# A hybrid encoder block on one core: q and k rows interleaved, and the second MLP stage in a written order on the first stage's tiles

## The chip, the core and the metric

The kernel runs on one core of a Trainium2 chip. Five engines work side by side, each through its own instructions in order: PE (TensorE: matmul), DVE (VectorE), ACT (ScalarE), POOL (GpSimd) and SP (SyncE, which here only issues transfers). They wait for each other through semaphores. The metric is the device time in microseconds (us); lower is better.

## The reference, cut to what matters

One layer on x of 1024 tokens by 1024 features, all in float32:

```python
h = rmsnorm(x, norm_mix_w)
z, xbc, dt_raw, q, k, v = jnp.split(h @ w_in, offs, axis=-1)
y_ssm = ssd_mixer(z, xbc, dt_raw, ...)            # conv, two-way chunked scan, gate, norm
y_na = neighbourhood_attention(q, k, v, ...)      # 16 heads of 64, q and k normed per head
x = x + jnp.concatenate([y_ssm, y_na], -1) @ w_out
h = rmsnorm(x, norm_mlp_w)
return x + jnp.square(jax.nn.relu(h @ w_mlp_in)) @ w_mlp_out   # 1024 -> 4096 -> 1024
```

In the attention each token sees a window of 8 rows by 16 columns of the 16 x 64 grid, with a bias per head.

## The kernel before, in words

**Number format.** Every float32 operand of a matmul is split into a high part (`hi`, made by ACT at L369) and a low part (`lo`, made by DVE or POOL at L370 as the difference), and a product is three matmuls: hi·hi, hi·lo, lo·hi. The helper `split_to(hl, src, eng)` does one such split of a 128 x 1024 tile; `eng` says who makes the low part. Weights are split with POOL, activations with DVE.

**Stages in time.** 0 to about 200 us: the norm of x, projections of x, B, C, dt, convolution. Up to about 610 us: the pieces of z, q, k, v and the scan. About 610 to 890 us: attention, interleaved with the first three quarters of the output projection. About 890 to 975 us: its last quarter, the second norm and the first blocks of the MLP. About 975 to 1270 us: the first MLP matmul (stage 1). From then to the end: the second (stage 2).

**Attention.** It goes over 8 pairs of heads, p = 0 to 7, in two rounds of tiles (`q0`/`q1`, and so on). q, k and v were stored to DRAM by the projection stage (ACT's queue issues those stores) and `pair_loads` (L412 on) brings a pair back: q in 4 transfers of 256 KB, each to 64 partitions, one per half of the tile and of the parts (hi, lo); k in 2 transfers of 512 KB, each to 64 partitions (head j to partitions 64j to 64j+63); the low part of k, `kl`, in 2 of 256 KB to 64 partitions; v in one of 1 MB to 128 partitions. For a head the tile `q[:, j]` holds on its 128 partitions one block of 64 rows with the high part and one with the low part, and `k[:, j]` the same rows of k twice, so that one matmul (L1401) sums two of the three terms; a second one with `kl` (L1402), whose other half is zero (set by POOL at L442, in the first round), adds the third. Scores `psc` are shifted by a bias `mb` and their maxima taken (DVE, L1405), exponentiated (ACT, L1417), turned by PE (L1429), split (`pth`, ACT L1441; `ptl`, DVE L1439) and multiplied with v (L1369). The bias comes from DRAM (`braw`) and is added to a mask by POOL (L1336). The output weights `wraw` are loaded by SP (L500) and split by ACT (`wh`, L507) and POOL (`wl`, L510) for the projection matmuls `po` (L364 to L366).

**What sets the order up to 975 us.** A planner takes tasks with a cost for their engine, tiles, readers and due times and makes a list; `in_order()` fixes each engine's instructions in the order of that list. A load is one task on SP (`load_task`), so all loads, of whatever tile, have the line L397.

**The MLP.** Each stage is a blocked product of 2 x 2 blocks done with 7 products instead of 8 (`ORD = (1, 2, 6, 5, 7, 3, 4)`); sums and differences of blocks are made by DVE. Stage 1 has 8 blocks `fb` of 512 hidden features. A product is 24 matmuls. `Block.split(i)` makes the differences of the weights it needs and splits one tile; `Block.product(i)` issues the matmuls; `Block.sums(i)` takes the PSUM results (ACT copies, L1628, or DVE adds, L1633), applies relu and square (ACT, L1639) and, for products 3 and 4, makes the combinations that stage 2 wants (DVE, L1646 to L1654) and stores them to `act_dr`. Stage 2 has 4 parts of 7 products, 48 matmuls each: two tiles of weights and two of activations are needed for a product. Weights are loaded to `wraw` tiles and combined by DVE (L1915, L1916, L1918, L1920); activations are loaded (`ar`) and split (`ahl`, with DVE); the PSUM results are added to `acc`, which starts as the residual x2 (L1945). After stage 1 the pool `b0s` is closed, and stage 2 opens pools of its own. From 975 us on, a scheduler of the compiler's front end sets the order on each engine; nothing in the kernel's text fixes it.

Of the kernel before, what the change touches and what calls it, by code (L numbers as in the profile page):

```python
# [10 lines left out]
F32 = mybir.dt.float32  # L11
# [219 lines left out]
def hymba_block(  # L231
# [64 lines left out]
    q_dr = dr.tile([2, 2, 4, P, T], F32, name="q_dr")  # L296
# [113 lines left out]
    def pair_loads(plan, p, after=()):  # L410
# [4 lines left out]
        qp = {(j, a): part(q) for j in range(2) for a in range(2)}  # L415
        kp = [part(k) for _ in range(2)]
        for j in range(2):
            for a in range(2):
                load_task(
                plan,  # L420
                    256,
                    partial(lambda j, a: q.t[a * HD : (a + 1) * HD, j].bitcast(F32), j, a),
                    partial(lambda j, a: q_dr[p // 4, a ^ j, p % 4, j * HD : (j + 1) * HD], j, a),
                    reads=after, writes=[qp[j, a]],
                    name="q",
                    since=-10.0 if p == 1 else -1e3,
                )
            load_task(
                plan,
                512,  # L430
                partial(lambda j: k.t[j * HD : (j + 1) * HD].bitcast(F32), j),
                partial(lambda j: k_dr[p // 4, 0, p % 4].rearrange("(h d) t -> d h t", h=2), j),
                reads=after, writes=[kp[j]],
                name="k",
                **free,
            )
        if p < 2:
            kls[p] = Buf(f"kl{i}"), []
            for j in range(2):
                half_, whole = part(kls[p][0]), kls[p][0]  # L440
                kls[p][1].append(half_)
                task("POOL", 1.0, partial(lambda j, b: nc.gpsimd.memset(b.t[HD * (1 - j) : HD * (2 - j), j].bitcast(F32), 0.0), j, whole), writes=[half_], name="kl0", **free)  # L442
        kl, klp = kls[i]
        for j in range(2):
            hp = slice(HD * j, HD * j + HD)
            load_task(plan, 256, partial(lambda hp, j: kl.t[hp, j].bitcast(F32), hp, j), partial(lambda hp: k_dr[p // 4, 1, p % 4, hp], hp), reads=after, writes=[klp[j]], name="kl", **free)
# [11 lines left out]
    def handed_on(plan, loaded):  # L458

        Buf, part = plan.buf, plan.part  # L460
        q, k, kl, v = (plan.given(Buf(b.tag), b.t) for b in (loaded[0], loaded[2], loaded[4], loaded[6]))
        qp = {(j, a): part(q) for j in range(2) for a in range(2)}
        kls[0] = kl, [part(kl) for _ in range(2)]
        return q, qp, k, [part(k) for _ in range(2)], *kls[0], v
# [56 lines left out]
    with ExitStack() as ph:  # L521
# [375 lines left out]
        def piece(j, b):  # L897
# [28 lines left out]
            to, w = (q_dr, 80) if kind(j) == "q" else (k_dr, 81)  # L926
# [6 lines left out]
            def turn():  # L933
                for i in range(4):
# [10 lines left out]
                    to[g, :, :, :, s].rearrange("a p f t -> f (a p) t"),  # L945
# [242 lines left out]
        def in_order():  # L1188
# [4 lines left out]
            for ins in traced[start:]:  # L1193
                if ins.engine in behind:
# [49 lines left out]
    with ExitStack() as ph:  # L1244
# [107 lines left out]
        def attend(H, mb, loaded, yT, yparts, den, dens):  # L1352
# [39 lines left out]
            for b in range(NT):  # L1392
# [51 lines left out]
                task("PE", 2 * (n / 2400 + 0.014), scores, reads=[qp[hh, 0], qp[hh, 1], *kp, klp[hh]], writes=[pt], due=due(b), name="psc")  # L1444
# [101 lines left out]
    with ExitStack() as ph:  # L1546
# [283 lines left out]
        for fb in range(8):  # L1830
# [13 lines left out]
    b0s.close()  # L1844

    with ExitStack() as ph:
        phase["ps"] = ph.enter_context(
            tc.tile_pool(name="ps4", bufs=1, space=PSUM, reuse_waits="tile")
        )
        ra, wa_, rb, x0, wb_, a2, a1, arb = (  # L1850
            ph.enter_context(tc.tile_pool(name=n, bufs=1, side="right", reuse_waits="tile"))
            for n in ("ra", "wa", "rb", "x0", "wb", "a2", "a1", "arb")
        )
        x1, a3 = (
            ph.enter_context(tc.tile_pool(name=n, bufs=1, reuse_waits="tile")) for n in ("x1", "a3")
        )
        acc = [p.tile([P, NT // 2, D], F32, name="acc") for p in (x0, x1)]
        hls[:] = [wa_] * 2 + [wb_] * 2 + [wp] * 3
        raw_a = [arp] * 2 + [ra] * 4
        raw_b = [rb] * 6 + [wp] * 2  # L1860
        raw_x = [arp] * 2 + [arb] * 2
        ahl = [a1] * 2 + [a2] * 2 + [a3] * 2
        for n in ("hl", "raw", "rb", "ar", "ahl"):
            ring[n] = 0

        def raw_of(n):
            if n in ("11", "21"):
                return ring_tile("raw", raw_a, ("wraw",), (F32,))[0]
            return ring_tile("rb", raw_b, ("wraw",), (F32,))[0]

        def a_load(fb, i, u):
            ar = ring_tile("ar", raw_x, ("ar",), (F32,))[0]
            nc.sync.dma_start(
                ar.rearrange("p (a t) -> p a t", a=2), act_dr[fb][i - 1, :, 2 * u : 2 * u + 2, :]
            )
            return ar

        def a_split(ar):
            pool = ahl[ring["ahl"] % 6]
            ring["ahl"] += 1  # L1880
            t = pool.tile([P, 2, 1024], F32R, tag="ahl", name="ahl", bufs=2)
            split_to((t[:, 0], t[:, 1]), ar, nc.vector)
            return t[:, 0], t[:, 1]

        for fb in range(4):
            bq = [{}, {}]
            for n in ("11", "21", "12", "22"):
                for q in bq:
                    q[n] = raw_of(n)
            first = {}  # L1890
            with ExitStack() as order:
                if fb == 1:
                    order.enter_context(tc.issue_after(begun.ins))
                for n in ("11", "21", "12", "22"):
                    for u in range(2):
                        r0 = (2 * fb + u) * 512 + (int(n[0]) - 1) * 256
                        d0 = (int(n[1]) - 1) * 512
                        nc.sync.dma_start(
                            bq[u][n].rearrange("p (a d) -> p a d", a=2),
                            w_mlp_out[0][r0 : r0 + 256, d0 : d0 + 512].rearrange(  # L1900
                                "(a p) d -> p a d", p=P
                            ),
                        )
                    if n in ("11", "21"):
                        i = 1 if n == "11" else 2
                        first[i] = [a_load(fb, i, u) for u in range(2)]
            X = [ps_mm("px2") for _ in range(4)]
            Y = [ps_tp("py2"), ps_tp("py2"), ps_s("py2"), ps_s("py2")]
            for i in ORD:
                wa = []  # L1910
                for u in range(2):
                    q = bq[u]
                    if i == 6:
                        q["t1"], q["t2"] = raw_of("t1"), raw_of("t2")
                        nc.vector.tensor_tensor(q["t1"], q["12"], q["11"], op=sub)  # L1915
                        nc.vector.tensor_tensor(q["t2"], q["22"], q["t1"], op=sub)  # L1916
                    elif i == 7:
# [77 lines left out]
```

## Time and profile before

| | |
|---|---|
| time, median of 3 runs | 1585.77 us (1585.5 to 1588.29) |
| the profiled execution | 1589.21 us, of which the span from the first to the last instruction is 1587.4 us |
| busy, share of the span | PE 98%, PEld 81%, DVE 64%, POOL 46%, ACT 45% |
| mean granted clock of PE | 0.992 |
| moved by DMA | 278.73 MB, mean 176 GB/s |

PE is TensorE's matmul, PEld its weight load, which overlaps PE. In a row of a timeline the first number is the start in us, the second the duration; `out<-in` are the program's names, and `[3.17 <-POOL wl L510]` says that the engine sat idle for 3.17 us before it and what ended that. In a row of the windows view each engine has its busy time and the number of its instructions; then come the granted clock (1.00 is full speed), the mean busy share of the 16 DMA engines (records can overlap, so it may pass 1) and the rate in GB/s.

### The profile page before, as it was taken

How to read it: one execution, taken by the hardware profiler on the slowest of the kernel's cores; microseconds unless marked ns; L12 is line 12 of the kernel's file. 1: busy time of each engine (PE TensorE's matmuls, PEld its weight loads, DVE VectorE, ACT ScalarE, POOL GpSimd, SP SyncE). 2: the span in 40 equal slices, each digit the busy share in tenths (PEclk: the TensorE clock that was granted, in tenths of full speed). 3: DMA queues.
4: the chain of work that ended last, by engine and by line, in shares of the span. 5: the costliest groups of instructions: out<-in, count | busy, mean ns of one | idle time of the engine just before them, and what ended most of it. 6: DMA issues, size and time to landing. Idle time of an engine off the chain costs nothing. (4 is left out here: it accounts for less than half of the span.)

```text
span 1587.4 us, 20805 instructions
## 1 busy us (share of the span) xinstructions
PE 1548.1 (98%) x7462; PEld 1291.3 (81%) x7462; DVE 1013.5 (64%) x1414; ACT 720.9 (45%) x1187; POOL 730.3 (46%) x530
## 2 busy tenths in 40 slices
PE   7999999999999999999999998999999999999999
PEld 5788878888878888788888886888888778888887
DVE  3776444687688854567776475444444579787863
ACT  5444323444345435567686244554454444333330
POOL 2000066774779832233364353444444555555450
PEclk9999999999999999999999999999999989999999
DMA  8212398777777795978792422444443486443332
GB/s 225 54 40 70 89 311 262 231 238 248 230 209 214 225 278 172 257 208 227 193 238 94 159 94 93 174 158 146 151 155 120 159 306 251 159 161 131 107 106 80
DMA packets 184226, 278.73 MB, mean 176 GB/s; under 512 B 14819, under 2 KB 106043, under 8 KB 184123
## 3 DMA queue, kind: packets, MB, share of 16 engines
q1 hardware_dynamic: 133323, 233.88, 48.2%
q10 hardware_dynamic: 49792, 39.85, 7.6%
q0 software_dynamic: 1008, 3.67, 0.6%
q8 instruction: 59, 0.97, 0.3%
q14 instruction: 44, 0.36, 0.1%
HBM read 191.51 MB, written 89.18 MB: 177 GB/s over the span
## 5 line engine op out<-in xcount | busy, mean ns | idle before, releaser
L370 POOL TENSOR_TENSOR wl<-wraw,wh 128x1024 fp32r<-128x1024 f32 x113 | 308.7, 2743 | 305.5 <-ACT wh L369 305.5
L364 PE MATMUL pq<-wh,hTh 128*128 128x512 f32 x512 | 204.9, 400 | 2.3 <-DVE qn L931 1.7
L366 PE MATMUL pq<-wh,hTl 128*128 128x512 f32 x512 | 199.9, 390 | 0.0
L365 PE MATMUL pq<-wl,hTh 128*128 128x512 f32 x512 | 199.7, 390 | 0.1
L369 ACT ACTIVATE wh<-wraw 128x1024 fp32r<-128x1024 f32 x125 | 131.4, 1055 | 143.5 <-PE px L1221 40.1
L1221 PE MATMUL px<-wh,ahl 128*128 128x512 f32 x512 | 163.1, 395 | 4.6 <-ACT ahl L369 3.1
L1221 PE MATMUL px<-h,wh 128*128 128x512 f32 x512 | 160.1, 394 | 2.7 <-DVE cq L1633 2.7
L370 DVE TENSOR_TENSOR ahl<-ar,ahl 128x1024 fp32r<-128x1024 f32 x56 | 117.0, 2094 | 22.4 <-ACT ahl L369 21.5
L369 ACT ACTIVATE ahl<-ar 128x1024 fp32r<-128x1024 f32 x56 | 58.5, 1052 | 160.3 <-PE px L1221 80.6
L1221 PEld LDWEIGHTS px<-wh,ahl 128*128 128x128 f32 x512 | 97.6, 191 | 26.7 <-ACT ahl L369 3.6
L1221 PEld LDWEIGHTS px<-h,wh 128*128 128x128 f32 x512 | 96.6, 190 | 22.9 <-DVE cq L1633 3.1
L364 PEld LDWEIGHTS pq<-wh,hTh 128*128 128x128 f32 x512 | 96.2, 188 | 21.8 <-DVE qn L931 2.1
L366 PEld LDWEIGHTS pq<-wh,hTl 128*128 128x128 f32 x512 | 96.1, 188 | 20.8
L365 PEld LDWEIGHTS pq<-wl,hTh 128*128 128x128 f32 x512 | 96.3, 188 | 18.9 <-DVE wl L884 0.5
L1221 PE MATMUL px<-wl,ahl 128*128 128x512 f32 x256 | 101.3, 396 | 0.0
L1221 PE MATMUL px<-h,wl 128*128 128x512 f32 x256 | 100.4, 392 | 0.0
L1439 DVE TENSOR_TENSOR ptl<-ptp,pth 128x384 fp32r<-128x384 f32 (+1 forms) x128 | 65.4, 520 | 37.5 <-ACT pth L1441 36.5
L1405 DVE CUSTOM_DVE_ANT_0 pr<-psc,mb 128x384 f32<-128x384 f32 (+1 forms) x128 | 65.7, 520 | 26.6 <-PE psc L1402 23.5
L1417 ACT ACTIVATE pr<-pr,nmx 128x384 f32<-128x384 f32 (+1 forms) x128 | 74.6, 584 | 17.3 <-DVE nmx L1405 16.8
L1221 PE MATMUL pz<-h,wh 128*128 128x512 f32 x256 | 80.3, 395 | 0.8 <-DVE h L1763 0.8
L364 PE MATMUL po<-wh,yh 128*128 128x512 f32 x192 | 80.1, 417 | 0.2 <-DVE x L1327 0.2
L1221 PE MATMUL pz<-wh,ahl 128*128 128x512 f32 x256 | 80.1, 389 | 0.0
(332 smaller groups left out, 3743.4 us busy)
## 6 DMA issues: line engine op xcount, KB each, us to landing
ar<-act_dr SPq DMA_DIRECT2D x56, 512.0 KB, 4.4
act_dr<-cq SPq DMA_DIRECT2D x49, 512.0 KB, 3.0
wraw<-in_w_in_dram SPq DMA_DIRECT2D x44, 512.0 KB, 6.3
rb<-cum_dr SPq DMA_DIRECT2D x32, 512.0 KB, 6.1
wraw<-in_w_mlp_in_dram SPq DMA_DIRECT2D x32, 512.0 KB, 5.2
wraw<-in_w_mlp_out_dram SPq DMA_DIRECT2D x32, 512.0 KB, 5.6
q_dr<-hl ACTq DMA_DIRECT2D x16, 512.0 KB, 5.6
k_dr<-hl ACTq DMA_DIRECT2D x16, 512.0 KB, 3.6
```

The costliest lines, as they stand in the source:

```text
L364: nc.tensor.matmul(pt, lhsT=ah, rhs=bh, start=first, stop=False)
L365: nc.tensor.matmul(pt, lhsT=ah, rhs=bl, start=False, stop=False)
L366: return nc.tensor.matmul(pt, lhsT=al, rhs=bh, start=False, stop=last)
L369: nc.scalar.activation(hl[0], src, AF.Copy)
L370: eng.tensor_tensor(hl[1], src, hl[0].bitcast(F32), op=sub)
L1221: nc.tensor.matmul(pt, lhsT=a, rhs=b, start=f, stop=l, skip_group_check=True)
L1405: nc.vector.tensor_tensor_reduce(pr.t[:, 0:n], pt.t[:, 0:n], mb.t[:, o : o + n], scale=-1.0, scalar=3.0e38, op0=add, op1=ALU.min, accum_ou ...
L1417: nc.scalar.activation(pr.t[:, 0:n], pr.t[:, 0:n], AF.Exp, bias=nmx.t[:, b : b + 1], scale=-1.0, accum_out=den.t[:, hh, b : b + 1],)
L1439: nc.vector.tensor_tensor(lo[0], pv3, hi.bitcast(F32), op=sub)
```

## The change

It has two parts.

**q and k interleaved.** In DRAM the array of q is now [2, P, 2, 4, T]: for each feature row d the high and low part lie beside each other. In SBUF row d of a head's part a lies on partition 2d + a. So q comes in 2 transfers of 512 KB to all 128 partitions (per pair), instead of 4 of 256 KB to 64. k, which has to stand on both rows of each d, comes in 4 transfers of 256 KB, each to every second partition (`k.t[a:P:2, j]`), instead of 2 of 512 KB to 64 neighbouring ones; `kl` goes to the even partitions, and POOL zeroes all 128 partitions of its tile instead of 64. The bytes are the same, and so is the count of a pair's issues. The scores task of a head (`scores`) now waits for that head's q, k and `kl` alone; before, it waited for both heads' k. The store of q by ACT goes to the new places.

**The MLP stages.** Stage 2 has no pools of its own: its tiles take the tags of stage 1 (the activations h1 to h3, h4 and h7, the attention tiles, the `cq` tiles and the weight rings), and it stays in the same PSUM pool. `in_order` now takes engines to leave out, and the last block of stage 1 with all of stage 2 stands in an order written by hand for PE, DVE, ACT and POOL; SP's is left to the scheduler. Splits are made two products ahead: while product n is issued, `ready(n + 2)` hands out its steps (the differences of weights, the activations' split, the weights' split) between the product's four groups of matmuls. The first splits of stage 2 are set between the steps of the last block of stage 1, and the differences `t1` and `t2` for stage 2's third product stand after that block's last product. There is one more tile kind for `t1`, `t2` (before they took `wraw` tiles).

```diff
-    q_dr = dr.tile([2, 2, 4, P, T], F32, name="q_dr")
+    q_dr = dr.tile([2, P, 2, 4, T], F32, name="q_dr")
...
-                    partial(lambda j, a: q.t[a * HD : (a + 1) * HD, j].bitcast(F32), j, a),
-                    partial(lambda j, a: q_dr[p // 4, a ^ j, p % 4, j * HD : (j + 1) * HD], j, a),
...
-                partial(lambda j: k.t[j * HD : (j + 1) * HD].bitcast(F32), j),
-                partial(lambda j: k_dr[p // 4, 0, p % 4].rearrange("(h d) t -> d h t", h=2), j),
...
+                partial(lambda j: q.t[:, j].bitcast(F32), j),
+                partial(lambda rows: q_dr[p // 4, rows, :, p % 4].rearrange("d a t -> (d a) t"), rows),
...
+            for a in range(2):
...
+                    partial(lambda j, a: k.t[a:P:2, j].bitcast(F32), j, a),
+                    partial(lambda rows: k_dr[p // 4, 0, p % 4, rows], rows),
...
-                task("POOL", 1.0, partial(lambda j, b: nc.gpsimd.memset(b.t[HD * (1 - j) : HD * (2 - j), j].bitcast(F32), 0.0), j, whole), writes=[half_], name="kl0", **free)
+                task("POOL", 1.3, partial(lambda j, b: nc.gpsimd.memset(b.t[:, j].bitcast(F32), 0.0), j, whole), writes=[half_], name="kl0", **free)
...
-            load_task(plan, 256, partial(lambda hp, j: kl.t[hp, j].bitcast(F32), hp, j), partial(lambda hp: k_dr[p // 4, 1, p % 4, hp], hp), reads=after, writes=[klp[j]], name="kl", **free)
+            load_task(plan, 256, partial(lambda j: kl.t[0:P:2, j].bitcast(F32), j), partial(lambda rows: k_dr[p // 4, 1, p % 4, rows], rows), reads=after, writes=[klp[j]], name="kl", **free)
...
-                task("PE", 2 * (n / 2400 + 0.014), scores, reads=[qp[hh, 0], qp[hh, 1], *kp, klp[hh]], writes=[pt], due=due(b), name="psc")
+                task("PE", 2 * (n / 2400 + 0.014), scores, reads=[qp[hh], kp[hh], klp[hh]], writes=[pt], due=due(b), name="psc")
...
-        for fb in range(8):
+        for fb in range(7):
...
+        rings = {
+            "ahl": [over(hA, f"h{i}{n}") for i in (1, 2, 3) for n in range(2)],
+            "hl": [over(b0, t) for t in ("k", "v", "kl")] + [of_wp] * 3,
+            "raw": [over(arp, "wraw", F32), over(hq, "q", F32)],
+            "ar": [over(arp, "ar", F32), over(b0, "q", F32)],
+            "t": [over(hA, f"h7{n}", F32) for n in range(2)],
+        }
...
+        kb, o = Block(7), Part(0)
...
+        with in_order(skip=(mybir.EngineType.SP,)):
...
+            kb.product(5)
+            o.split_w(1, 0)
+            kb.sums(5)
...
+            kb.product(7)
+            o.split_w(1, 1)
+            o.split_w(2, 0)
+            kb.sums(7)
+            kb.product(3)
+            o.split_a(2)
+            o.split_w(2, 1)
+            kb.sums(3)
+            kb.product(4)
+            o.change(6, 0)
+            o.change(6, 1)
+            kb.sums(4)
+            load_acc(0)
+            row = [(o, i) for i in ORD] + [(p, i) for p in map(Part, range(1, 4)) for i in ORD]
+            for n, (o, i) in enumerate(row):
+                ahead = iter(row[n + 2][0].ready(row[n + 2][1], n > 0) if n + 2 < len(row) else ())
+                for _ in o.product(i):
+                    next(ahead, None)
...
+    b0s.close()
```

PE's instructions stand in the same order in both kernels but for the attention, where a few groups change places. Two other places matter.

DVE at the end of stage 1, before. L1633 adds a PSUM result of block 7 (`px`, `py`, `pz` are PSUM tiles), L1915, L1916 and L1918 are the differences of weights of stage 2, L1646 to L1654 the combinations of block 7, L370 a split's low part, L1945 the first add of stage 2:

```order
L1633 TENSOR_TENSOR cq<-cq,py_11010 128x512
L1915 TENSOR_TENSOR wraw<-wraw 128x1024 x2
L1633 TENSOR_TENSOR cq<-cq,px_10963 128x512
L1916 TENSOR_TENSOR wraw<-wraw 128x1024
L1918 TENSOR_TENSOR wraw<-wraw 128x1024
L1916 TENSOR_TENSOR wraw<-wraw 128x1024
L1918 TENSOR_TENSOR wraw<-wraw 128x1024
L1633 TENSOR_TENSOR cq<-cq,px_10964 128x512
L1633 TENSOR_TENSOR cq<-cq,pz_11079 128x512
L1633 TENSOR_TENSOR cq<-cq,pz_11080 128x512
L1646 TENSOR_TENSOR cq<-cq 128x1024
L1648 TENSOR_TENSOR cq<-cq 128x1024
```

The same place after. L1639 is the add that was L1633, L1916 and L1917 are `t1` and `t2`, L1593 belongs to block 7 itself:

```order
L1639 TENSOR_TENSOR cq<-cq,py_11033 128x512
L370 TENSOR_TENSOR ahl<-ar,ahl 128x1024 x2
L1593 TENSOR_TENSOR wraw<-wraw 128x1024
L1639 TENSOR_TENSOR cq<-cq,px_10963 128x512
L1639 TENSOR_TENSOR cq<-cq,px_10964 128x512
L370 TENSOR_TENSOR ahl<-ar,ahl 128x1024 x2
L1639 TENSOR_TENSOR cq<-cq,pz_11107 128x512
L1639 TENSOR_TENSOR cq<-cq,pz_11108 128x512
L1652 TENSOR_TENSOR cq<-cq 128x1024
L1654 TENSOR_TENSOR cq<-cq 128x1024
L1656 TENSOR_TENSOR cq<-cq 128x1024
L1916 TENSOR_TENSOR wt<-wraw 128x1024
```

The differences of stage 2's weights have moved behind all the adds of block 7, and the first two pairs of activation splits ahead of the last ones.

SP in the attention, at the loads of one pair, before and after:

```order
L397 DMA k<-k_dr 64x2x1024 x2
L397 DMA q<-q_dr 64x1024 x4
L397 DMA kl<-k_dr 64x1024
L397 DMA braw<-t_dr 128x384
L397 DMA rd_dr<-rd 16x128
L397 DMA v<-v_dr 128x8x256
```

```order
L397 DMA k<-k_dr 64x1024
L397 DMA q<-q_dr 128x1024
L397 DMA k<-k_dr 64x1024
L397 DMA q<-q_dr 128x1024
L397 DMA kl<-k_dr 64x1024
L397 DMA braw<-t_dr 128x384
L397 DMA v<-v_dr 128x8x256
L397 DMA k<-k_dr 64x1024 x2
```

The k loads now come one per head and per parity; the second head's k stands behind the bias and v.

More of the change, by code (lines that the diff above doesn't have):

```diff
@@ L461, in handed_on @@
         q, k, kl, v = (plan.given(Buf(b.tag), b.t) for b in (loaded[0], loaded[2], loaded[4], loaded[6]))
[L462 removed]
+        qp = [part(q) for _ in range(2)]
         kls[0] = kl, [part(kl) for _ in range(2)]
@@ L925, in piece @@
             qn, sq, rq, tp = Buf("qn"), Buf("sq"), Buf("rq"), Buf("tp")
-            to, w = (q_dr, 80) if kind(j) == "q" else (k_dr, 81)
+            w = 80 if kind(j) == "q" else 81
             col = pcol[:, w : w + 1]
@@ L1843, in hymba_block @@
                 kb.sums(i)
[L1844 to L1894, printed above, removed]
-                    for u in range(2):
[L1896 to L1917, printed above, removed]
-                        nc.vector.tensor_tensor(q["12"], q["22"], q["12"], op=sub)
-                    elif i == 4:
-                        nc.vector.tensor_tensor(q["21"], q["21"], q["t2"], op=sub)
-                    src = q[{1: "11", 2: "21", 3: "22", 4: "21", 5: "t1", 6: "t2", 7: "12"}[i]]
-                    ar = first[i][u] if i in first else a_load(fb, i, u)
-                    wa.append((a_split(ar), w_split(src, nc.gpsimd)))
-                if fb == 0 and i in (1, 6):
-                    h = i == 6
-                    for t in range(4):
-                        begun = nc.sync.dma_start(acc[h][:, t, :], x2_dr[4 * h + t])
-                if i == 5:
-                    Y = [ps_tp("pz2"), ps_tp("pz2"), ps_s("pz2"), ps_s("pz2")]
-                for t in range(4):
-                    pt = (X if i in (1, 6, 7, 4) else Y)[t]
-                    ts = slice(t * P, t * P + P)
-                    for u in range(2):
-                        (ah, al), (wh, wl) = wa[u]
@@ new lines, in over, with of_wp @@
+        def over(pool, tag, dt=F32R):
+            return lambda name: pool.tile([P, 2, 1024], dt, tag=tag, name=name, bufs=4 if pool is hq else 1)
+        def of_wp(name):
+            return [wp.tile([P, 1024], F32R, tag=t, name=t, bufs=3) for t in ("wh", "wl")]
+        rings = {
[5 more added lines that the diff above has]
+        }
@@ L1949, in hymba_block, with load_acc @@
                         )
+                    yield
+        def load_acc(h):
+            for n in range(2):
+                acc[2 * h + n] = t = over(*((hA, f"h4{n}"), (hq, "q"))[h], F32)("acc")
+                for m in range(2):
+                    last_ = nc.sync.dma_start(t[:, m], x2_dr[4 * h + 2 * n + m])
+            return last_
+        kb, o = Block(7), Part(0)
+        kb.load("12", "21", "22")
+        kb.tiles()
+        o.load("11")
+        o.load_a(1)
+        o.load("21")
+        with in_order(skip=(mybir.EngineType.SP,)):
+            kb.split(1)
+            kb.split(2)
+            kb.split(6)
+            kb.product(1)
+            kb.sums(1)
+            kb.split(5)
+            kb.product(2)
+            kb.sums(2)
+            kb.split(7)
+            kb.product(6)
+            o.split_a(1)
+            kb.sums(6)
+            o.load_a(2)
+            kb.split(3)
+            kb.product(5)
+            o.split_w(1, 0)
+            kb.sums(5)
+            o.load("12")
+            o.load("22")
+            kb.split(4)
+            kb.product(7)
[16 more added lines that the diff above has]
+                    next(ahead, None)
+                if n == 1:
+                    begun = load_acc(1)
+                    tc_after = begun.ins
+                if i == 5 and o.fb < 3:
+                    row[n + 4][0].load_all(tc_after if o.fb == 0 else None)
+    b0s.close()
     arps.close()
```

124 lines of the change are left out of this document (105 added, 19 removed).

## The prediction

> **What bounds the kernel now.** The page first, then PE's waits, then the places where they lie. The page's first line says who sets the time, and the chain of waits says how it ends:
>
> ```profile
> PE 1548.1 (98%) x7462; PEld 1291.3 (81%) x7462; DVE 1013.5 (64%) x1414; ACT 720.9 (45%) x1187; POOL 730.3 (46%) x530
> ...
> 1333.33 10.88 PE pz L1221 x48
> ...
> 1583.61 0.69 DVE acc L1945
> ```
>
> PE is busy in 98% of the span, so only PE's holes, and the matmuls that run at a lower clock, can be won: no edit here takes a matmul away. 48 matmuls in 10.88 us are 226.7 ns each. The waits view lists where PE stood still:
>
> ```profile
> PE po L365 <- POOL wl L510: 3.9, 2, 3.2
> PE pv L1369 <- ACT pth L1441: 3.3, 1, 3.3
> ...
> PE px L1221 <- ACT ahl L369: 3.1, 1, 3.1
> ...
> PE px L1221 <- DVE cq L1633: 2.7, 1, 2.7
> ```
>
> The first two lie in the attention, the others where stage 1 of the MLP passes into stage 2: the two places that the change touches. The windows view shows what each loses (matmuls in brackets behind PE's busy time; then the granted clock, the DMA share, GB/s):
>
> ```profile
> core 0: us, PE busy (x) PEld busy (x) DVE busy (x) ACT busy (x) POOL busy (x), PEclk, DMA share, GB/s
> 625.00:650.00 25.00, 24.24 (x145) 20.75 (x144) 19.18 (x53) 17.71 (x49) 6.42 (x7) 1.00 1.06 264
> 650.00:675.00 25.00, 21.27 (x122) 18.31 (x120) 13.21 (x37) 11.45 (x31) 7.88 (x8) 1.00 1.04 252
> 675.00:700.00 25.00, 22.15 (x129) 19.93 (x130) 16.58 (x43) 16.98 (x46) 7.46 (x7) 0.93 0.89 257
> 700.00:725.00 25.00, 24.95 (x150) 21.99 (x148) 17.98 (x49) 17.27 (x48) 9.61 (x9) 1.00 0.70 166
> ...
> 1250.00:1275.00 25.00, 19.19 (x72) 15.01 (x71) 20.32 (x12) 13.09 (x15) 18.17 (x9) 0.87 0.52 186
> 1275.00:1300.00 25.00, 24.17 (x95) 19.16 (x94) 21.40 (x19) 10.61 (x12) 13.04 (x9) 0.86 0.79 273
> ```
>
> In the attention 150 matmuls go through in an undisturbed 25 us. From 625 to 700 there are 145 + 122 + 129 = 396 instead of 450: 54 short, at 25/150 us each **9.0 us lost**, and just there the DMA engines are full (share 1.06, 1.04). That 9.0 is the ceiling of the first part of the change.
>
> **Part one: the loads of q and k.** What does a load to 64 partitions cost against one to 128? Two stretches in which little else moves:
>
> ```profile
> 714.00:724.00 10.00, 10.00 (x63) 8.85 (x61) 6.86 (x21) 7.19 (x20) 4.37 (x4) 1.00 0.98 221
> 726.00:732.00 6.00, 6.00 (x40) 5.22 (x39) 5.40 (x13) 5.36 (x15) 4.80 (x4) 1.00 1.07 394
> ```
>
> ```profile
> 712.81 1.27 SPq L397 DMA_DIRECT2D k<-k_dr  x2
> 714.17 2.47 SPq L397 DMA_DIRECT2D q<-q_dr  x4
> ...
> 721.50 0.37 SPq L397 DMA_DIRECT2D v<-v_dr  x1
> ```
>
> From 714 to 724 the pair's k and q go to 64 partitions each: engines full (0.98), 221 GB/s. From 726 to 732 v and the activations go to 128: engines full, 394 GB/s. A pair's q, k and `kl` are 1 + 1 + 0.5 MB, 2.62 million bytes: 11.9 us at 221, 6.7 at 394. So each pair frees up to 5.2 us of the queue.
>
> [...] Whether every second partition counts as a span of all is a rival below; no run here shows it.
>
> Which stalls hang on that queue?
>
> ```profile
> 672.67 0.50 PE L365 MATMUL po<-wl,yh 128*128 128x512 f32 x1 [3.17 <-POOL wl L510]
> ...
> 677.74 0.48 PE L1369 MATMUL pv<-pth,v 128*128 128x256 f32 x1 [3.29 <-ACT pth L1441]
> ...
> 667.93 2.38 POOL L1336 TENSOR_TENSOR mb<-braw,nam 128x384 f32<-128x384 f32 x3 [9.68 <-DVE nmx L1405]
> 670.28 2.33 POOL L510 TENSOR_TENSOR wl<-wraw,wh 128x1024 fp32r<-128x1024 f32 x1
> ...
> 676.26 1.06 ACT L507 ACTIVATE wh<-wraw 128x1024 fp32r<-128x1024 f32 x1 [10.26 <-DMA wraw<-in_w_out_dram]
> 677.22 0.47 ACT L1441 ACTIVATE pth<-ptp 128x384 fp32r<-128x384 f32 x1
> ...
> 666.28 0.38 SPq L500 DMA_DIRECT2D wraw<-in_w_out_dram  x1
> ```
>
> *The second stall (3.29 us)*: the weights issued at 666.28 landed at 676.2, 10 us later; ACT stood at their split for 10.26 us, and `pth`, for which PE waited, was queued right behind it. 512 KB at 394 GB/s are 1.3 us, so the rest was queue. The rate in that window, 252, lies near 221: by it (394 - 252)/(394 - 221), some 80%, of the engines' time went to 64-partition loads, and such a load's time shrinks by 44%. So the landing comes some 3.5 us earlier and ends the stall: 3.29 us. *The clock behind it*: 0.93 in 675 to 700 is 0.07 x 25 = 1.7 us, and goes with it. *The first stall (3.17)*: POOL's `wl` stood behind the bias addition, which by the trace was released by DVE, not by a transfer; DVE, however, was itself at a pace that the loads set. I count half, 1.5. Sum **6.5 us**. Bounds: nothing (the stall is only passed on to another load) and 9.0.
>
> What the part adds:
>
> ```profile
> L442 POOL MEMSET kl<- x4: 947/948/951, 559.9 to 622.1; 64x1024 f32 x4
> q_dr<-hl ACTq DMA_DIRECT2D x16, 512.0 KB, 5.6
> ```
>
> The four zeroings now take 128 partitions; even at twice 0.95 us they are 3.8 us of POOL up to 622, ahead of the lossy stretch, while POOL is busy 6.42 of 25 us in the first window above. k has 4 issues instead of 2 and q 2 instead of 4: at 1.27 for two and 2.47 for four, SP's time is equal. ACT's stores of q go to other places; ACT only issues them, and a store that took twice its 5.6 us would delay the first pair alone. All three count as nothing; uncovered, the zeroing and the store would be 4 and 6 us once.
>
> **Part two: stage 1 to 2.** The timeline there, PE first:
>
> ```profile
> 1261.74 0.39 PE L1221 MATMUL px<-h,wl 128*128 128x512 f32 x1
> 1264.82 1.12 PE L1221 MATMUL px<-h,wh 128*128 128x512 f32 x2 [2.69 <-DVE cq L1633]
> ...
> 1272.55 0.79 PE L1221 MATMUL px<-wh,ahl 128*128 128x512 f32 x1 [3.12 <-ACT ahl L369]
> ...
> 1277.16 1.22 PE L1221 MATMUL px<-wh,ahl 128*128 128x512 f32 x2 [0.83 <-DVE ahl L370]
> ...
> 1288.66 0.39 PE L1221 MATMUL py<-wh,ahl 128*128 128x512 f32 x1
> ```
>
> ```profile
> 1259.62 3.42 DVE L1916 TENSOR_TENSOR wraw<-wraw 128x1024 f32<-128x1024 f32 x1
> ...
> 1264.09 0.67 DVE L1633 TENSOR_TENSOR cq<-cq,px 128x512 f32<-128x512 f32 x1
> ...
> 1249.53 12.42 POOL L370 TENSOR_TENSOR wl<-wraw,wh 128x1024 fp32r<-128x1024 f32 x4 [3.03 <-ACT wh L369]
> ...
> 1271.45 1.99 ACT L369 ACTIVATE ahl<-ar 128x1024 fp32r<-128x1024 f32 x2
> ```
>
> From 1261.97, where the even spacing ends, to 1288.66 PE issues 12 matmuls of product 4 and 48 of stage 2's first: 60 x 0.2267 = 13.6 us; it takes 26.7. **13.1 us lost**: stalls 2.69 + 3.12 + 0.83 = 6.6, and the clock of the two windows above, (0.13 + 0.14) x 25 = 6.75. The cause stands in DVE's rows: the differences of stage 2 (3.42 us each, beside POOL's splits) come before the add at 1264.09 that frees PSUM for product 4, and everything behind is late, down to the first `ahl` at 1271.45.
>
> The written order puts those differences behind block 7's adds and the first two activation splits well ahead. Are its own deadlines met? With block 7's first product at 0, products take 5.44 us (24 matmuls), so stage 2 begins at 38.1, its second product at 49.0, its third at 59.8. POOL makes block 7's and stage 2's low parts in one line at 12.42/4 = 3.1 us each: the last for block 7 is done at about 31.6 and is due at 32.6 (the tight one), the first pair for stage 2 at about 34 (due 38.1), the second at 39 (due 49.0). `t1`, `t2` on DVE run from 44 to 49 if `acc` has landed by 46: it takes the tile of h4, so it is loaded when product 4 ends at 38.1, and 2.1 million bytes at 394 GB/s are 5.3 us. That is the change's new wait: behind DVE's first add into `acc` stand the activation splits of the third product, and for those PE waits; the third product's splits are done by 57, due at 59.8. From there the load on the engines decides:
>
> ```profile
> 1288.66:1584.00 295.34, 294.21 (x1297) 243.05 (x1295) 216.60 (x188) 98.33 (x100) 144.59 (x49) 1.00 0.44 152
> L370 DVE TENSOR_TENSOR ahl<-ar,ahl 128x1024 fp32r<-128x1024 f32 x56 | 117.0, 2094 | 22.4 <-ACT ahl L369 21.5
> L1945 DVE TENSOR_TENSOR acc<-acc,px 128x512 f32<-128x512 f32 x64 | 42.5, 678 | 28.3 <-PE px L1221 28.3
> ```
>
> DVE is busy 216.6 of 295.3 us, POOL 144.6, PE lost 1.1 there. Two products' lead is 21.8 us, enough for one late operation of 3.4. I take **13.3 us** (13.1 and a little of the 1.1). Bounds: 14.3 (no hole from 1262 to the end) and 6 (the stalls' half returns at the tight splits). The tail, from the last add on, is the same.
>
> [...]
>
> **Sum.** 13.3 + 6.5 = 19.8. The profiled execution took 1589.2 us, so 1569.4; the runs' median lies 3.4 lower, so **1566.0 us**.
>
> **Rivals.**
> 1. *The attention's stalls stay.* For it: the first stall was ended by DVE, not by a load; a load more early may only move a stall to POOL's queue. Against it: full DMA engines at just that place. Only part two: 1585.8 - 13.3 = 1572.5.
> 2. *The k loads don't do what is meant*: every second partition is no faster than 64 in a row, and only q's 1 MB of the 2.5 is. A pair then takes 1.57 MB at 221 and 1.05 at 394: 7.1 + 2.7 = 9.8 us instead of 6.7, 2.1 won instead of 5.2. The weights' 10 us shrink by 2 or so; the second stall, 3.29, goes in part: gain 2.5, time 1570. Nothing in the trace speaks for or against.
> 3. *The tight splits stall.* One deadline missed by 1 us brings back the low clock too (above, 6.6 us of stalls cost as much again). Half of part two, 6.6: 1572.7; with the attention's stalls too: 1579.
> 4. *Slower: DVE becomes the bound of stage 2.* Adds take 4 x 7 x 4 = 112 times 0.68, 76 us. 56 splits and 32 differences share the other 229 of four parts (4 x 76.2 = 305 us): 2.6 us each. Beyond that mean PE waits in every part. The splits' mean is 2.09 now, 3.4 in the worst place. If the written order sets them beside POOL's splits as a rule and the mean becomes 2.85, DVE needs 327 us: 22 us over, all gains gone, 1588; at 3.0, 1601. Against it: POOL is busy less than half of the stage.
>
> **How the numbers follow.** The forecast (both parts as summed) 0.48; rivals 1 and 2 0.15 and 0.15; rival 3 0.15 (a third of it with the attention's stalls); rival 4 0.04; no difference, by a mix of 1 and a worse 3, 0.03. The likeliest's own range is 1562 (14.3 + 9.0 = 23.3 won) to 1569. The range takes in rivals 1, 2 and the milder 3: 1560.5 (some of the small holes elsewhere too) to 1576. A difference under 0.2% (3.2 us) can't be told from none here: all but rival 4 and that mix, less 0.02 for rival 3 gone worse, are faster: faster 0.91, same 0.05, slower 0.04.
>
> **What would show it.** Right: no PE wait on `pth` or `wl` over 1 us from 625 to 700 and some 440 or more matmuls there; a rate near 390 GB/s while a pair's q and k move; no wait on `cq` or `ahl` at the passage, and clock 1.00 there; 60 matmuls over it in about 14 us. Wrong: a rate that stays near 220 while k moves (rival 2); POOL's split of block 7's last product ending after its product is due, with PE waiting on `wl` (rival 3); DVE over 90% busy in stage 2 with PE waiting on `ahl` in every part (rival 4).

## The result and the profile after

The median went from 1585.63 us (1583.2 to 1588.29) to **1566.0 us** (1564.51 to 1567.14); the ratio is 0.9875 with a 95% interval of 0.9857 to 0.9894. The span of the profiled execution went from 1587.4 to 1563.6 us.

The first line of the page after, and two of PE's waits (the largest, and the only one left on `wl`; us in total, times, longest; line numbers are those of the changed kernel):

```profile
PE 1540.4 (99%) x7462; PEld 1287.2 (82%) x7462; DVE 1001.5 (64%) x1414; ACT 725.4 (46%) x1187; POOL 717.0 (46%) x530
```

```profile
PE ptn L579 <- DMA xt<-in_x_dram: 4.0, 4, 2.0
...
PE po L365 <- POOL wl L512: 0.7, 1, 0.7
```

The waits for `pth`, `cq` and `ahl` are gone, and the one for `wl` lies at 884.78 us, behind the stretch that lost time before. The windows over the two places say the same:

```profile
625.00:650.00 25.00, 24.98 (x155) 22.17 (x154) 20.22 (x57) 18.92 (x53) 7.48 (x8) 1.00 0.87 313
650.00:675.00 25.00, 25.00 (x151) 22.38 (x150) 17.71 (x48) 17.30 (x48) 9.40 (x9) 1.00 0.87 272
675.00:700.00 25.00, 25.00 (x150) 22.22 (x149) 18.14 (x49) 16.83 (x45) 9.74 (x9) 1.00 0.74 255
...
1250.00:1275.00 25.00, 25.00 (x112) 20.69 (x111) 22.68 (x15) 11.97 (x13) 16.13 (x12) 1.00 0.91 310
1275.00:1300.00 25.00, 24.96 (x110) 20.37 (x109) 20.72 (x22) 10.16 (x10) 10.87 (x5) 1.00 0.93 363
```

155 + 151 + 150 matmuls stand where there were 396, and at the passage 112 and 110 where there were 72 and 95, all at full clock. While one pair's q, k and `kl` move, the rate is

```profile
674.00:679.00 5.00, 5.00 (x31) 4.38 (x30) 3.31 (x10) 4.01 (x10) 1.45 (x1) 1.00 0.95 333
```

333 GB/s instead of 221 (311 at the next pair, 703.5 to 709). The loads of k and `kl` to every second partition are among them. Had only q become faster, the second rival's sum gives 2.62 MB in 9.8 us, 267 GB/s. The 333 is a mean over the start too: from 676 us on, three microseconds move 381, 361 and 401 GB/s, the last of them

```profile
678.00:679.00 1.00, 1.00 (x7) 0.86 (x6) 0.98 (x4) 0.62 (x3) 1.00 (x1) 1.00 0.99 401
```

That is as fast as the 394 of transfers to 128 partitions before, so here the transfers to every second partition were not held to the 221 of those to 64 neighbouring ones.

### The profile page after: what moved, and what is told of

Its sections match the earlier page's. It is cut to its first block, busy times and chain, and to the rows that moved or that the text cites. A ratio compares the mean times of both kernels' runs of the same rounds, so it can differ in the third digit from the quotient of the medians.

```text
span 1563.6 us, 20789 instructions
## 1 busy us (share of the span) xinstructions
PE 1540.4 (99%) x7462; PEld 1287.2 (82%) x7462; DVE 1001.5 (64%) x1414; ACT 725.4 (46%) x1187; POOL 717.0 (46%) x530
## 4 chain that ended last, share of the span: by engine, by line
PE 88%; DMA 3%; DVE 3%; issue 2%; POOL 2%; ACT 1%; SPq 1%; ACTq 0%; DVEq 0%; POOLq 0%
PE px L1227 22%; PE pz L1227 11%; PE pq L364 6%; PE pq L366 6%; PE pq L365 6%; PE py L1227 5%; PE po L364 3%; PE po L365 3%; PE po L366 3%; PE px L366 3%; PE pv L1375 3%; PE px L364 3%; PE px L365 3%; PE ptp L1435 2%; PE pd L1132 2%
## 5 line engine op out<-in xcount | busy, mean ns | idle before, releaser
L370 POOL TENSOR_TENSOR wl<-wraw,wh 128x1024 fp32r<-128x1024 f32 x76 | 193.3, 2547 | 203.9 <-ACT wh L369 200.6
L369 ACT ACTIVATE wh<-wraw 128x1024 fp32r<-128x1024 f32 x88 | 92.6, 1059 | 141.6 <-PE px L1227 29.1
L370 DVE TENSOR_TENSOR ahl<-ar,ahl 128x1024 fp32r<-128x1024 f32 x56 | 108.5, 1977 | 7.3 <-ACT ahl L369 7.3
L1227 PE MATMUL px<-whl,ahl 128*128 128x512 f32 x408 | 96.5, 389 | 0.0
L1227 PEld LDWEIGHTS px<-whl,ahl 128*128 128x128 f32 x408 | 76.6, 188 | 15.9
L370 POOL TENSOR_TENSOR whl<-wraw,whl 128x1024 fp32r<-128x1024 f32 x21 | 58.3, 2786 | 62.7 <-ACT whl L369 50.2
L1227 PE MATMUL px<-wh,ahl 128*128 128x512 f32 x240 | 77.9, 390 | 0.0
```

The lines of the kernel that those rows point to most:

```text
L369: nc.scalar.activation(hl[0], src, AF.Copy)
L370: eng.tensor_tensor(hl[1], src, hl[0].bitcast(F32), op=sub)
L1227: nc.tensor.matmul(pt, lhsT=a, rhs=b, start=f, stop=l, skip_group_check=True)
```

## The experiments

**The kernel before, once more**, for a second profile; no edit.

> The kernel before once more, for a second profile. Theory: the same stalls at the same places: PE waits for wl and pth in the attention (3 us each, 9 us short between 625 and 700 us) and for cq and ahl at the passage of the MLP stages (13 us). If a stall is missing, its share of the gain changes from one execution to the next, and the 3.6 us by which the first profiled execution lies above the median may be that.

Its one time was 1584.61 us. The same three windows, the split of the late weights on ACT and PE's longest wait in the attention:

```profile
625.00:650.00 25.00, 24.24 (x146) 20.79 (x145) 18.78 (x52) 18.47 (x50) 5.64 (x7) 1.00 1.06 279
650.00:675.00 25.00, 22.06 (x126) 18.97 (x124) 14.01 (x40) 12.84 (x33) 8.94 (x9) 1.00 1.05 265
675.00:700.00 25.00, 24.64 (x142) 22.20 (x143) 18.90 (x49) 17.20 (x50) 9.50 (x9) 0.93 0.93 258
```

```profile
673.67 1.06 ACT L507 ACTIVATE wh<-wraw 128x1024 fp32r<-128x1024 f32 x1 [6.88 <-DMA wraw<-in_w_out_dram]
...
670.73 0.50 PE L365 MATMUL po<-wl,yh 128*128 128x512 f32 x1 [0.46 <-POOL wl L510]
675.16 0.39 PE L1369 MATMUL pv<-pth,v 128*128 128x256 f32 x1 [2.65 <-ACT pth L1441]
```

414 matmuls instead of 450: 36 short, 6.0 us lost, where the first profile had lost 9.0. So the hole in the attention has no fixed size, and the first profile had a large one. The wait for `wl`, 3.17 us in the first profile, is 0.46 here.

**Each part alone.** The first kernel has the change of q and k only, the second that of the MLP only:

```diff
# q and k alone: the diff's hunks up to the scores task
-    q_dr = dr.tile([2, 2, 4, P, T], F32, name="q_dr")
+    q_dr = dr.tile([2, P, 2, 4, T], F32, name="q_dr")
...
# the MLP alone: the diff's other hunks
-        for fb in range(8):
+        for fb in range(7):
...
+        with in_order(skip=(mybir.EngineType.SP,)):
```

> The kernel before with the q and k part alone; the MLP stages as before. Theory (two parts that add up): only the attention changes. Its 9.0 to 10.4 us of lost time (9.0 counted in the windows of before, 10.4 between the first score and the last output projection of the two profiles) are won, so 1575.5 to 1579 us, the passage between the MLP stages costs its 13 us as before. Rival 1 (only the passage pays): within 0.2% of 1585.6. Rival 2 (only q is faster): about 1583.

> The kernel before with the MLP part alone; q and k as before. Theory: 13.1 to 14 us are won, 1571.5 to 1573, and the two stalls in the attention (3.2 and 3.3 us) stand as before. If both parts were one gain counted twice (for instance because the profile of before was an unlucky execution), it would come out with e1 to more than the 19.6 us of the change: e1 and e2 together should win 19.6 within 2 us.

Against a median of 1584.25 for the kernel before: q and k alone 1579.46 us (ratio 0.9971, 0.9962 to 0.9981), 4.8 less; the MLP alone 1571.24 (0.9916, 0.9890 to 0.9943), 13.0 less. The second is just under the 1571.5 to 1573 expected, the first a little over the 1575.5 to 1579: the whole hole was counted there too. Together 17.8, against 18.3 for both (1584.25 - 1566.0): the parts add up, as far as the MLP part's interval, 8 us wide, can tell. The passage with q and k alone (a window, then two rows of PE's waits), and then windows of the kernel with the MLP alone:

```profile
1250.00:1275.00 25.00, 16.76 (x57) 12.39 (x56) 20.77 (x14) 14.44 (x16) 15.59 (x12) 0.80 0.71 244
```

```profile
PE px L1225 <- ACT ahl L369: 4.7, 1, 4.7
PE px L1225 <- DVE cq L1637: 2.7, 1, 2.7
```

```profile
650.00:675.00 25.00, 24.70 (x143) 21.46 (x141) 17.10 (x48) 16.24 (x43) 11.38 (x10) 1.00 1.00 268
675.00:700.00 25.00, 25.00 (x152) 22.45 (x151) 18.93 (x51) 16.85 (x49) 7.42 (x9) 1.00 0.99 272
1250.00:1275.00 25.00, 25.00 (x112) 20.71 (x111) 22.67 (x16) 13.64 (x15) 16.14 (x12) 1.00 0.86 287
1275.00:1300.00 25.00, 24.96 (x111) 20.33 (x110) 20.72 (x21) 8.73 (x9) 10.06 (x5) 1.00 1.03 396
```

The passage is closed by the MLP part alone. In the attention this second kernel has the loads of before, and in its profile hardly a hole: from 625 to 700 us 146 + 143 + 152 = 441, 9 short, 1.5 us. The profiled execution is the fastest of its four, 1567.86 us; the others go up to 1575.09, while the changed kernel's four lie within 2.6 us. With one experiment more below there are four profiles of the old attention. How long ACT stood at the late weights (its wait at L507) goes with what PE lost:

| profile with the loads of before | ACT's wait for the weights | PE's wait for `pth` | matmuls short, 625 to 700 | lost |
|---|---|---|---|---|
| the kernel before, first | 10.26 | 3.29 | 54 | 9.0 |
| the kernel before, second | 6.88 | 2.65 | 36 | 6.0 |
| with one dependency (below) | 5.95 | 2.07 | 24 | 4.0 |
| the MLP part alone | 3.59 | none | 9 | 1.5 |

The mean loss is 5.1 us, which is what q and k alone won (4.8). So the way the prediction followed, from the weights' load to ACT's queue to `pth` to PE, is borne out by its size from execution to execution. What differs from one execution to the next is mostly when that load goes out. In the first profile SP issued it at 666.28, 2.5 us after ACT's split ahead of it (663.80); in the one of the MLP part alone at 662.08, 2.4 us before that split (664.46). From the issue to the split that waited for it, it took 10.0 and 8.2 us. So of the 6.7 us between the two waits of ACT, 4.9 lie in the issue and 1.8 in the transfer. What shortens the wait is another question.

**Is it the rate of the loads?** Two kernels cut each load of q, k and `kl` in two. In one each piece goes to partitions 0 to 63 or 64 to 127, in the other each piece takes half of the columns over all 128. Bytes, pieces and the order on PE, DVE, ACT and POOL are the same in the two. The diff is in short: `<-` stands for the load of the right side into the left, and k and `kl` are cut likewise.

```diff
-  q.t[:, j]                       <- q_dr[p // 4, rows, :, p % 4]
+  q.t[HD * c : HD * (c + 1), j]   <- q_dr[p // 4, j * HD + 32 * c : j * HD + 32 * (c + 1), :, p % 4]     # by partitions, c = 0, 1
+  q.t[:, j, 512 * c : 512 * (c + 1)] <- q_dr[p // 4, rows, :, p % 4, 512 * c : 512 * (c + 1)]            # by columns
```

> The kernel after, with each load of q, k and kl cut in two by partitions: every piece goes to partitions 0 to 63 or 64 to 127 (q all 64, k and kl every second of them). The next run has the same pieces, bytes, issues and order on every engine, but cut by columns, so each piece spans 0 to 127. Theory (the span of partitions sets the rate): here the rate while a pair moves falls from some 330 GB/s back towards 221, and the attention's holes come back: 1.5 to 9 us more than the run cut by columns. Rival (the gain is from finer dependencies and transfers): no difference between the two.

> The kernel after, with each load of q, k and kl cut in two by columns, each piece over all 128 partitions (k and kl on every second one). Theory: packets of 2 KB instead of 4 and 7 issues more per pair cost SP 4 us per pair, which is free; 1566 within 2 us, rate above 300 GB/s while a pair moves. Rival: as the run cut by partitions.

By partitions 1573.72 us (0.9931, 0.9914 to 0.9948), by columns 1571.46 (0.9923, 0.9903 to 0.9944). The pieces by partitions are 2.3 us slower, on the side of the theory, but the single times overlap (1572.24 to 1575.63, and 1569.18 to 1577.47). Against expectation both are slower than the changed kernel. The reason is not how the pieces are cut: as more and smaller tasks the planner gave another order, with new holes in both kernels at the same places:

```profile
700.00:725.00 25.00, 22.43 (x137) 19.11 (x136) 18.93 (x50) 18.22 (x49) 9.01 (x9) 1.00 0.82 220
```

```profile
700.00:725.00 25.00, 22.43 (x140) 19.14 (x139) 18.25 (x46) 17.87 (x47) 9.71 (x9) 1.00 0.71 229
```

The first is cut by partitions, the second by columns: 22.43 us of PE in both. So the comparison says little, and the pair was run again with the two pieces inside one task, which leaves the order of the changed kernel on PE, DVE, ACT and POOL row for row:

```diff
-        emit = lambda: nc.sync.dma_start(out(), src())
+        def emit():
+            for c in range(len(out) if type(out) is list else 1):
+                nc.sync.dma_start(*((out[c](), src[c]()) if type(out) is list else (out(), src())))
...
```

> The kernel after with its own order kept on PE, DVE, ACT and POOL; each load of q, k and kl is issued as two, one to partitions 0 to 63 and one to 64 to 127. Theory (the rate of the loads holds up the attention): against the next run, which differs only in how the pieces are cut, 1.5 to 6 us slower, with holes between 625 and 700 us. Rival (with the order and the dependencies of after, the slower loads are hidden): the same within 1.5 us, and the attention's gain came from what a head waits for and from the order.

> As the run before, but each load is cut in two by columns, so that each piece spans all 128 partitions. Both theories: 1566 within 2 us, 450 or more matmuls from 625 to 700 us; the cost of 7 more issues per pair on SP, about 4 us, is hidden.

By partitions 1565.84 us (0.9889, 0.9874 to 0.9905; single times 1563.81 to 1570.66), by columns 1564.49 (0.9878, 0.9865 to 0.9892). The windows, by partitions and then by columns:

```profile
625.00:650.00 25.00, 24.98 (x153) 22.07 (x152) 20.55 (x57) 18.52 (x51) 6.54 (x7) 1.00 1.02 304
650.00:675.00 25.00, 25.00 (x152) 22.41 (x151) 17.68 (x49) 17.11 (x47) 10.37 (x10) 1.00 0.99 285
```

```profile
625.00:650.00 25.00, 24.98 (x154) 22.19 (x153) 20.14 (x56) 18.74 (x53) 8.61 (x9) 1.00 0.88 294
650.00:675.00 25.00, 25.00 (x152) 22.30 (x151) 17.41 (x47) 16.88 (x45) 8.29 (x8) 1.00 0.92 283
```

The pieces by partitions keep the DMA engines full (1.02 and 0.99 against 0.88 and 0.92 for about the same GB/s), and there is no hole all the same. 1.35 us lies between the medians, and the two ranges overlap. Full engines alone don't make the hole, then, in this order. The run doesn't bring back the whole of the old slowness: the share per GB/s in the first window was 1.06/264 before, 1.02/304 by partitions, 0.88/294 by columns, so about a third of the way from after's kind of loads back to before's.

**Is it what a head waits for?**

```diff
-                task("PE", 2 * (n / 2400 + 0.014), scores, reads=[qp[hh], kp[hh], klp[hh]], writes=[pt], due=due(b), name="psc")
+                task("PE", 2 * (n / 2400 + 0.014), scores, reads=[qp[hh], *kp, klp[hh]], writes=[pt], due=due(b), name="psc")
```

> The kernel after, with one line changed back: a head's scores wait for both heads' k. The loads keep their full rate. Theory (rate): 1566 within 1.5 us. Rival (what a head waits for): 2 to 6 us slower, with holes in the attention; the planner's order changes with it, as it did between before and after.

1565.56 us (0.9882, 0.9868 to 0.9895): no effect, though the planner's list changes in places with it. What is left beside the rate is the planner's order. In the changed kernel's profile the same two splits of weights lie like this on ACT, beside SP's issue of the second one's load:

```profile
662.83 1.06 ACT L509 ACTIVATE wh<-wraw 128x1024 fp32r<-128x1024 f32 x1
...
676.42 1.05 ACT L509 ACTIVATE wh<-wraw 128x1024 fp32r<-128x1024 f32 x1
...
660.92 5.85 SPq L502 DMA_DIRECT2D wraw<-in_w_out_dram  x2
```

Before, the load was issued at 666.28 and ACT reached its split with four instructions of work behind the split at 663.80. Now the first of the two loads goes out at 660.92, and ACT has other work until 676.42: the load has 15 us of room, where it had none. It landed in 5.1 us, and the 10 us of before would have done as well. The old loads in the new order were not tried, since the order comes out of the loads' tasks and the tiles' layout out of the loads; how much of the 4.8 us is the order and how much the rate stays open.

**The MLP: order or shared tags?** The text of the change without the written order, so that the scheduler sets it:

```diff
-        with in_order(skip=(mybir.EngineType.SP,)):
+        with ExitStack():
```

> The kernel after, with the shared tags and the text of the last block and of stage 2 kept, but without the written order: the scheduler sets it again on all engines. Theory (the order wins): the scheduler again puts differences of stage 2 ahead of block 7's adds (in its order t1 stands before the second add of product 7), so at least 6 of the 13 us come back: 1572 to 1580. Rival (the shared tags win, because stage 2 no longer waits for pools to close): within 2 us of 1566.

1570.39 us (0.9908, 0.9888 to 0.9928), 4.4 above the changed kernel: less came back than the 6 us expected. The passage itself stays closed (112 and 111 matmuls in its two windows); the loss has moved 50 us on. There PE waits, ahead of the first part's seventh product and of the second part's first, for DVE's adds into `acc` (L1967), which free PSUM; they stand behind differences of the second part (L1917, L1919) and activation splits:

```profile
1300.00:1325.00 25.00, 23.29 (x103) 19.03 (x102) 21.25 (x16) 7.92 (x8) 12.65 (x5) 1.00 0.69 269
1325.00:1350.00 25.00, 23.03 (x95) 18.62 (x95) 23.65 (x22) 9.02 (x10) 11.76 (x4) 0.93 0.44 149
```

```profile
PE px L1227 <- DVE acc L1967: 3.7, 2, 2.0
```

So shared tags and a text two products ahead, without any written order, win about two thirds of the 13 us, and the order the rest. The tags and the lead were not run apart from each other.

**The kernel before with one dependency**: `t1` and `t2` of stage 2's first part may not pass block 7's last difference of product 3 on DVE (the diff in short; the second line stands for a loop over the two).

```diff
+ last_sum[0] = nc.vector.tensor_tensor(c12, c11, c12, op=sub)      # in Block.sums(3)
...
+ if fb == 0:  tc.add_manual_dep(t.ins, last_sum[0].ins.name, ..., reason="issue_after")   # for t1 and t2 of both tiles
```

> The kernel before with one dependency more: the differences t1 and t2 of stage 2's first part may not come before the last combination of block 7's third product on DVE. Theory (these differences, ahead of block 7's adds on DVE, cause the whole passage's loss): the 2.7 us wait on cq is gone with its clock, the ahl wait shrinks; 1572 to 1579 us from 1584 to 1586. Rival (the first stage-2 splits are late for other reasons: pools that open late, ACT's own order): only the wait on cq goes, 1580 to 1583.

1590.17 us (ratio 1.0026, 1.0012 to 1.0040): slower, which neither theory allowed. The wait for `cq` did go. But now the differences stand between the splits:

```profile
1263.41 4.57 DVE L370 TENSOR_TENSOR ahl<-ar,ahl 128x1024 fp32r<-128x1024 f32 x2
1267.89 3.41 DVE L1918 TENSOR_TENSOR wraw<-wraw 128x1024 f32<-128x1024 f32 x1
...
1273.50 3.42 DVE L1930 TENSOR_TENSOR wraw<-wraw 128x1024 f32<-128x1024 f32 x1
1276.84 3.36 DVE L1655 TENSOR_TENSOR cq<-cq 128x1024 f32<-128x1024 f32 x1
1280.13 3.35 DVE L370 TENSOR_TENSOR ahl<-ar,ahl 128x1024 fp32r<-128x1024 f32 x1
...
1283.54 1.22 PE L1221 MATMUL py<-wh,ahl 128*128 128x512 f32 x2 [7.68 <-DVE ahl L370]
```

The stall went to the second product of stage 2 and grew to 7.68 us. DVE has more to do at this place than fits ahead of PE (from 1275 to 1300 us it is busy for all 25), and moving one item only passes the delay on. What helps is that the splits come first, in time for both products.

**The changed kernel with `t1`, `t2` where the scheduler had had them**:

```diff
+            o.change(6, 0)
+            o.change(6, 1)
             kb.sums(7)
...
-            o.change(6, 0)
-            o.change(6, 1)
             kb.sums(4)
```

> The kernel after, with t1 and t2 of stage 2's first part moved forward to where the scheduler had them: behind product 7 of block 7, ahead of its adds. Theory: PE waits again 2 to 4 us for cq with the low clock behind it: 1570 to 1575. Rival (their place doesn't matter, since the splits of stage 2's first two products already stand ahead of them): within 2 us of 1566.

1574.07 us (0.9938, 0.9914 to 0.9963), 8.1 more than the changed kernel, at the upper end of the 1570 to 1575 expected; the wait is longer than the 2 to 4 us named there:

```profile
1243.51 2.96 DVE L1916 TENSOR_TENSOR wt<-wraw 128x1024 f32<-128x1024 f32 x1 [6.49 <-PE px L1227]
1246.51 3.30 DVE L1917 TENSOR_TENSOR wt<-wraw,wt 128x1024 f32<-128x1024 f32 x1
1249.73 3.35 DVE L1916 TENSOR_TENSOR wt<-wraw 128x1024 f32<-128x1024 f32 x1
1253.12 1.23 DVE L1917 TENSOR_TENSOR wt<-wraw,wt 128x1024 f32<-128x1024 f32 x1
1254.26 1.28 DVE L1639 TENSOR_TENSOR cq<-cq,px 128x512 f32<-128x512 f32 x2
...
1255.09 1.19 PE L1227 MATMUL px<-h,wh 128*128 128x512 f32 x2 [6.17 <-DVE cq L1639]
```

Four differences ahead of one add: 10.75 us of DVE (1243.51 to 1254.26), a wait of 6.17 us for `cq`, and the clock at 0.86 behind it. The place of these four operations alone is worth 8 of the 13 us, once the splits are safe.

**A lead of one product instead of two**:

```diff
-                ahead = iter(row[n + 2][0].ready(row[n + 2][1], n > 0) if n + 2 < len(row) else ())
+                ahead = iter(row[n + 1][0].ready(row[n + 1][1], n > 1) if 0 < n < len(row) - 1 else ())
```

> The kernel after with the splits of stage 2 written one product ahead instead of two (the differences of a product's weights and its splits stand between the four groups of the product before it). Theory (the lead of two products is what lets the written order pass): three of seven products need differences, whose chain of two differences, a high part and two low parts (about 17 us from the first add, against 10.88) ends 6 us late, the others up to 2: 60 to 100 us slower. Rival (the written order is safe with any lead): within 5 us of 1566.

1593.17 us (1.0065, 1.0050 to 1.0081): 27 more than the changed kernel, and more than before, but well under the 60 to 100 expected. What shows are small waits, at product after product:

```profile
PE px L1227 <- DVE ahl L370: 10.5, 14, 1.4
PE px L1227 <- POOL wl L370: 5.8, 7, 0.8
PE px L1227 <- POOL whl L370: 3.3, 4, 0.8
```

They add up to 19.6 us and none is over 1.4, where the expectation had chains 6 us late; which step of the chain is shorter than the expected one was not traced, nor what makes up the rest of the 27 us. The sign was right: a written order with too short a lead is slower than the scheduler's.

## Why the prediction was right, point by point

- **What bounds the kernel.** PE's holes and its clock, at two places: right. The gain lies there, and the parts add up.
- **Part two, 13.3 us.** Measured 13.0 (the MLP part alone). The sum of stalls and clock from 1262 to 1289 us was the right term. *Its cause was told too simply.* The differences ahead of block 7's add are a cause (8.1 us when put back), but taking only them away made the kernel slower (1590.17); the splits had to come first as well, and about two thirds are won without a written order. "Everything behind is late" named as one cause what was two demands on the same DVE.
- **The deadlines.** The tight one named, block 7's last low part, held: no wait for `wl` there. `acc` was no trouble either. Another was tighter than written: the third product's activation splits. They were to be done at 57 us of block 7's clock for a need at 59.8. The first ended at 1276.74, 0.6 us after the product had started (its third matmul stood 0.2 us for it), the second at 1277.87, 0.4 us before the ninth matmul, the first that reads it. Hardly anything was left of the slack.
- **Part one, 6.5 us.** Measured 4.8. The mis-sized term is the whole hole of 9.0: it came from one execution, and three others show 6.0, 4.0 and 1.5. The second stall was traced rightly to the weights' load, but "the landing comes some 3.5 us earlier and ends the stall" credits the rate with too much. The second profile of the kernel before has just that: ACT's wait is 3.4 us shorter (6.88 instead of 10.26), and PE still waits 2.65 us for `pth` instead of 3.29, with the clock at 0.93 behind it. By this execution, a landing 3.5 us earlier is worth some 0.6 us of that stall. In the table above the stall is gone only with ACT's wait down to 3.59 us, 6.7 less than in the first profile; the new order, on which the prediction did not count, gave the load 15 us of room. A kernel with the new order and full DMA engines shows no hole either. The first stall, of which half was counted, was 0.5 us or nothing in the other profiles. The 394 GB/s in the sum are not the most of that trace, which moves 422 from 1005 to 1010 us, at a busy share of 1.03; with that rate the landing would come 4.0 us earlier instead of 3.5, which changes no term.
- **The step from profile to median, 3.4 us.** The profiled pair differs by 23.8 us of span, not by 19.8. Most of the 3.4 was that same large hole (9.0 against a mean of 5.1), so the forecast counted an average gain on an unusual execution. By the separate runs the parts are worth 17.8 us, 2.0 less than the 19.8 of the sum; the median of the kernel before lay between 1584.0 and 1585.6 us in the four series of runs, nearly as much as is left to explain. That the forecast meets the measured median to the tenth is luck: part one was 1.7 us too high, and the series of runs differ by about as much.
- **Rivals.** 1 (the attention's stalls stay): no; they go on average by 4.8. 2 (k no faster on every second partition): no, 333 GB/s where it has 267. 3: not here, but a lead of one product shows it, with 25 waits of at most 1.4 us each. The granted clock there was 1.00 in every 25 us from 1275 to 1550; the low clock that rival 3 expected behind a miss of 1 us did not show. 4 (DVE as the bound): no. Between 1288 and 1540 us PE lost nothing while DVE was busy 75% of the time:

```profile
1288.00:1540.00 252.00, 252.00 (x1113) 208.66 (x1113) 189.73 (x166) 93.67 (x93) 129.95 (x48) 1.00 0.42 139
```

## What to carry to other kernels

A stall of a transfer's making can differ from one execution to the next (here 1.5 to 9.0 us): take a second profile before its size goes into a sum. When one engine's queue holds more than fits ahead of a deadline, moving a single operation passes the stall on (here it grew to 7.68 us); write the order of the whole passage, first what the next two consumers need, and with a lead that covers a product's whole chain of differences and splits (a lead of one product cost 27 us here). And when a planner makes the order, a change of the tasks' shapes changes the order too, so an effect is a transfer's only if it stays with the order held fixed.

## What the runs showed of the hardware that was not expected

**A DVE split took 9.70 us beside four POOL splits in a row.** Before, a split on DVE beside POOL's splits took at most 3.4 us, and the prediction took that as its worst case. In the changed kernel this is one of two splits (DVE and, below, POOL at the same time):

```profile
1267.04 10.83 DVE L370 TENSOR_TENSOR ahl<-ar,ahl 128x1024 fp32r<-128x1024 f32 x2
...
1266.18 4.78 POOL L370 TENSOR_TENSOR wl<-wt,wh 128x1024 fp32r<-128x1024 f32 x2
1270.92 4.73 POOL L370 TENSOR_TENSOR whl<-wt,whl 128x1024 fp32r<-128x1024 f32 x2
```

```profile
L370 DVE TENSOR_TENSOR ahl<-ar,ahl x2: 1210/5453/9696, 1267.0 to 1276.7; 128x1024 fp32r<-128x1024 f32 x2
```

The second view gives the shortest, median and longest of the two: one took 1.21 us and the other 9.70, from 1267.04 to 1276.7, while four POOL splits ran back to back at 2.4 us each, as long as a split of the late weights on POOL in the attention (2.39 on average, before). The kernel with the MLP part alone and the one with the loads cut by columns in the same order show it at the same place (9.69 and 9.68 us); the one cut by partitions has one of 9.69 us, and the one without the written order one of 10.87 us. In the kernel before, four POOL splits in a row took 12.42 us (1249.53 to 1261.95), and four DVE operations, of 2.56, 0.67, 2.82 and 3.42 us, began and ended in that time. Why DVE's operations ended while POOL's splits were under way there, and DVE's split only after the fourth of them here (1276.74 against 1275.65; POOL's spans are rough), these runs don't tell.

**Every second partition was as fast as all.** Transfers of 64 partitions spread over all 128 moved, together with q's, at 333 GB/s, and at up to 401 once under way, where 64 neighbours each had 221 and all 128 had 394. k goes to 64 partitions per transfer in both kernels, and at 221 for k and 394 for q the rate would be 267, so here it went with the spread and not with the number of partitions.
